# Query and key tiles of the dilated attention: eight pairs by seven block products, six heads' outputs kept in memory outside the core

## The chip, the cores and the metric

The kernel runs on one core of one Trainium2 chip. The core has TensorE (matrix products), VectorE, ScalarE and GpSimd (called POOL in the profile) for elementwise work, and DMA queues, most of them issued from SyncE (SP). The metric is the device time of one execution in microseconds (us); lower is better.

## What is computed

A decoder trunk of two layers on 512 tokens of width 1024 in float32: layer 0 mixes tokens by dilated windowed attention, layer 1 by a state-space scan (Mamba-2), each is followed by a gated feed-forward layer with a short convolution, and all have a normalisation ahead. The change lies in the attention. Cut to that part, the reference is:

```python
qkv = (h @ w_qkv).reshape(bsz, s, N_ATTN_GROUPS, 3, ATTN_HEADS_PER_GROUP, ATTN_HEAD_DIM)
q = apply_partial_rope(qkv[:, :, :, 0], cos, sin)
k = apply_partial_rope(qkv[:, :, :, 1], cos, sin)
v = qkv[:, :, :, 2].astype(jnp.float32)
outs, lses = [], []
for g in range(N_ATTN_GROUPS):
    dil = ATTN_DILATIONS[g]
    o_g, lse_g = dilated_window_attention(q[:, :, g], k[:, :, g], v[:, :, g], dil,
                                          ATTN_WINDOWS[g] // dil)
    outs.append(o_g)
    lses.append(lse_g)
wts = jax.nn.softmax(jnp.stack(lses, axis=2), axis=2)
o = jnp.einsum("bsgh,bsghe->bshe", wts, jnp.stack(outs, axis=2))
return o.reshape(bsz, s, ATTN_OUT_WIDTH).astype(h.dtype) @ w_o
```

There are 3 groups (dilations 1, 4, 16) and 8 heads of 128 channels, so 24 query tiles and 24 key tiles, each 128 channels by 512 tokens, each the product of a 1024 x 128 weight with the normalised input.

## The kernel before, in words

Channels lie on the partitions and tokens along the free axis. A product in float32 is made of three matmuls in the rounded format float32r (`mm3`, lines 136 to 141): weight and input are each split in a high and a low part, and high x high, high x low and low x high are summed in a bank of PSUM. So one projection (`project`, line 147) takes 8 blocks of 128 input channels x 3 = 24 matmuls of 512 columns. The inputs `xh` and `xl` are 8 tiles each of 128 x 512.

`load_unit` brings a weight tile: a DMA from SP into `raw`, a ring of 4 tiles (pool `wr`, line 58), the high part by ScalarE (line 125) and the low part by VectorE (line 126) into `hi` and `lo`, rings of 5 tiles each (pool `wh`, line 59). Transfers and splits thus run some projections ahead of TensorE, as far as the rings are free.

Projections write to three banks of PSUM in turn (`mm_bank`); three more (`aux_bank`) hold transposes and values, and two (`side_bank`) hold scores. `qk_step` (from line 390) takes a query or key tile out of its bank: VectorE multiplies by a table of cosines that also holds the normalisation (line 395), shuffles 32 rows (line 398), and POOL does the sine part (lines 399 and 400).

The order on TensorE is written out by hand in `attend_and_project`: the scores of head h, its value transposes, two projections of head h + 1, the other scores and the join of the softmax pieces over dilations on VectorE (lines 462 to 479), then projections again, with the transposes of the weighted scores (line 488, tile pp, after their scaling on line 485) put behind the second of eight blocks of the sixth projection, and last the values (lines 496 and 501). On the other engines and on SP a planner orders instructions by its own estimate of times. Heads 6 and 7 and the output projection are mixed by the planner on TensorE too.

At the end of a head the output `o` (lines 523 to 525; one buffer) is split in a high and a low tile (lines 526 to 530), which stay until the output projection reads all eight heads. `high_low` (line 81) gives such tiles from two rings of 8.

At the start, `xp` tiles (the input, kept in the ring `v` of 12 tiles with the values) are split into xh and xl, while the first value projections `v_steps` run.

The feed-forward stage already computes its products by seven blocks (`load_sevens`, line 694, and `down_by_sevens`, line 728): two output tiles by two halves of the tokens, with the input blocks paired, are 2 x 2 block products, done with 7 multiplications in place of 8, at the cost of sums of weight blocks, of inputs and of results. Its matmuls have 256 columns.

Of the kernel before, what the change touches and what calls it, by code (L numbers as in the profile page):

```python
# [14 lines left out]
P = 128  # L15
# [16 lines left out]
FF_PARTS = ((0, 8), (8, 8), (16, 6))  # L32

# [18 lines left out]
def trunk(ctx: ExitStack, tc: tile.TileContext, A, out):  # L52
# [244 lines left out]

    vt = {}
# [55 lines left out]
    load2, second = v_steps(2, 0)  # L354
    with tc.manual_schedule(engines={mybir.EngineType.PE}):
        first[3]((0,))
        with tc.manual_schedule(engines={mybir.EngineType.DVE}):
            inv_rms(ssum, D, rcol, soon=True)
            load2(0)
        first[3]((1,))  # L360
        rb = along_free(rcol, "rb")
# [9 lines left out]
    dma(tri, A["tri"])  # L371
    with tc.manual_schedule(engines={mybir.EngineType.PE}):
        for f in second:
            f()
        T.matmul(warm[:, 0:P], ones, ones, start=True, stop=True)
# [26 lines left out]

    def v0_step(h):
        n = f"v0{h}"
        p = project(A["wqk"][h * 7 + 6], n)
        t = t2("t" + n, "vt", 1, s3)
        V.tensor_tensor(in_blocks(t), by_residue(p), by_residue(rbc), op=ALU.mult)
        v0[h] = t
# [9 lines left out]
    def qk_steps(h):  # L418
        steps = [lambda cut=None, g=g, c=c: qk_step(h, g, c, cut) for g in range(NG) for c in range(2)]
        return steps + [lambda: v0_step(h)]  # L420
# [4 lines left out]
    def attend(h):  # L425
# [99 lines left out]
        V.tensor_tensor(natural(o), natural(o), po.rearrange("p (n r l) -> p n r l", n=4, r=DIL), op=ALU.add)  # L525
        o_h, o_l = high_low(f"o{h}")
# [3 lines left out]
        ol.append(o_l)  # L530

# [22 lines left out]
    for f in qk_steps(0):  # L554
        f()
# [17 lines left out]
    for h in range(NH):  # L573
        if h < NH - 2:
            attend_and_project(h)
            if h == 3:
                for f in v_steps(1, 1)[1] + v_steps(2, 1)[1]:
                    f()
# [70 lines left out]
    H0, H1 = slice(0, 256), slice(256, 512)  # L649

# [42 lines left out]

    def load_sevens(src, name):

        def raw(t):
            return wr.tile([P, 1024], F32, tag="raw", name=f"raw{t}_{name}")

        a, b, c = (raw(t) for t in "abc")
        q = t2(f"q_{name}", "a", 13, lp)  # L700
        W0, W1 = slice(0, 512), slice(512, 1024)
        dma(a[:, W0], src[:, 0:512])
        dma(q, src[:, 512:1024])
        dma(b[:, W1], src[:, 1024:1536])
        dma(c[:, W0], src[:, 1536:2048])

        def sums(which=(0, 1)):
            if 0 in which:
                V.tensor_tensor(a[:, W1], q, b[:, W1], op=ALU.add)
                V.tensor_tensor(b[:, W0], a[:, W1], a[:, W0], op=ALU.subtract)  # L710
            if 1 in which:
                V.tensor_tensor(c[:, W1], c[:, W0], b[:, W0], op=ALU.subtract)
                V.tensor_tensor(q, a[:, W0], q, op=ALU.subtract)

        def split_weights(t, between=None):
            r = dict(zip("abcd", (a, b, c, q)))[t]
            hi, lo = (
                wh.tile([P, 1088], F32R, tag=k, name=f"{k}{t}_{name}")[:, 0 : r.shape[-1]] for k in ("hi", "lo")
            )
            SC.copy(hi, r)  # L720
            if between:
                between()
            V.tensor_tensor(lo, r, hi.bitcast(F32), op=ALU.subtract)
            return hi, lo

        return sums, split_weights
# [109 lines left out]
    def ffn(layer, done):  # L836
# [7 lines left out]
        for part, (c0, cn) in enumerate(FF_PARTS):  # L844
# [3 lines left out]
            def load(mp):  # L848
                return load_sevens(A["wds"][(layer * 2 + part) * 4 + mp], f"wd{layer}{part}{mp}")
# [580 lines left out]
def _layout(i):  # L1430
# [9 lines left out]
    w["wqk"] = np.concatenate([qk, v0], 1).reshape(56, P, D)  # L1440
    w["wv"] = (
# [60 lines left out]
```

## Time and profile before

| what | value |
|---|---|
| median of 3 runs | 1611.09 us (1610.67 to 1611.6) |
| the profiled execution | 1610.76 us |
| its span | 1608.8 us |
| TensorE busy | 1601.0 us |
| VectorE busy | 1164.2 us |
| ScalarE busy | 700.7 us |
| POOL busy | 567.9 us |
| granted TensorE clock, mean | 0.999 |
| one head of the attention (134.49 to 180.31 us) | 45.82 us |

In the rows that follow, PE is TensorE's matmuls, PEld its weight loads, DVE VectorE, ACT ScalarE. A row of a group gives line, engine, operation, result and inputs, shapes and count, then the busy time and the mean duration of one in ns, then the idle time of that engine ahead of it. A row of the chain gives start, length and what ran; a row of a stretch gives its bounds, its length and each engine's busy time in it. The profiled execution is 2.0 us longer than its span, which begins with the first and ends with the last instruction that the profile shows.

### The profile page before, as it was taken

What the parts mean: (1) busy time and instruction counts of PE and PEld (TensorE: products, weight loads), DVE (VectorE), ACT (ScalarE), POOL (GpSimd) and SP (SyncE); (2) the same over time, 40 slices, a digit from 0 to 9 for tenths busy, and PEclk for the clock granted to TensorE, in tenths of its full rate; (3) what the DMA queues carried; (4) which work ended last, traced back from release to release, by engine and by line L of the source; (5) the groups of instructions that cost most, each with busy time, mean ns of one, the idle gap of its engine ahead of it and who ended that gap; (6) DMA issues with size and microseconds to landing.
All of it is one profiled execution on the core that took longest, in us unless ns stands there. A gap on an engine that the chain in (4) does not pass through costs nothing.

```text
span 1608.8 us, 22680 instructions
## 1 busy us (share of the span) xinstructions
PE 1601.0 (100%) x8614; PEld 1392.8 (87%) x8614; DVE 1164.2 (72%) x1973; ACT 700.7 (44%) x1077; POOL 567.9 (35%) x432
## 2 busy tenths in 40 slices
PE   9999999999999999999999999999999999999998
PEld 8888888888888889989988888888888888988987
DVE  6366665276646878868758899988898687877864
ACT  5233333333324644443445455544444454444443
POOL 0444453055412653652331222222022285365230
PEclk9999999999999999999999999999999999999999
DMA  7322222222224323423323433233432322342331
GB/s 261 97 76 90 79 79 92 92 92 79 70 88 132 98 64 101 149 61 105 125 92 115 145 114 115 90 114 115 128 128 66 107 84 79 106 129 74 94 129 53
DMA packets 57853, 165.25 MB, mean 103 GB/s; under 512 B 6736, under 2 KB 10192, under 8 KB 57744
## 3 DMA queue, kind: packets, MB, share of 16 engines
q1 hardware_dynamic: 57184, 163.27, 31.5%
q8 instruction: 68, 1.11, 0.3%
q10 hardware_dynamic: 560, 0.53, 0.1%
q14 instruction: 41, 0.34, 0.1%
HBM read 161.62 MB, written 2.16 MB: 102 GB/s over the span
## 4 chain that ended last, share of the span: by engine, by line
PE 98%; DVE 1%; issue 0%; DMA 0%; POOL 0%; ACT 0%; POOLq 0%; DVEq 0%; SPq 0%; ACTq 0%
PE u L134 29%; PE qk L134 16%; PE v L134 8%; PE z L134 5%; PE wso L134 5%; PE xs L134 5%; PE wo L134 3%; PE b L134 3%; PE c L134 3%; PE wd L134 2%; PE wz L134 2%; PE py L1083 1%; PE pg L501 1%; PE pp L488 1%; PE po L496 1%; PE pf L1091 1%
## 5 line engine op out<-in xcount | busy, mean ns | idle before, releaser
L134 PE MATMUL u<-xh,hi_u 128*128 128x512 f32 x704 | 269.4, 383 | 0.0
L134 PE MATMUL u<-xh,lo_u 128*128 128x512 f32 x704 | 269.1, 382 | 0.0
L134 PE MATMUL u<-xl,hi_u 128*128 128x512 f32 x704 | 266.6, 379 | 0.0
L399 POOL TENSOR_TENSOR rotqk<-rotqk,sr 32x512 f32<-32x512 f32 x48 | 92.9, 1936 | 252.6 <-DVE rotqk L398 242.2
L134 PEld LDWEIGHTS u<-xh,lo_u 128*128 128x128 f32 x704 | 131.7, 187 | 24.6
L134 PEld LDWEIGHTS u<-xl,hi_u 128*128 128x128 f32 x704 | 131.7, 187 | 24.0
L126 DVE TENSOR_TENSOR lo_u<-raw_u,hi_u 128x1024 fp32r<-128x1024 f32 x88 | 123.8, 1415 | 37.6 <-ACT hi_u L125 37.6
L134 PEld LDWEIGHTS u<-xh,hi_u 128*128 128x128 f32 x704 | 131.7, 187 | 22.0 <-issue 0.4
L134 PE MATMUL qk<-xh,hi_qk 128*128 128x512 f32 x384 | 148.6, 387 | 0.0
L134 PE MATMUL qk<-xh,lo_qk 128*128 128x512 f32 x384 | 147.1, 383 | 0.0
L134 PE MATMUL qk<-xl,hi_qk 128*128 128x512 f32 x384 | 145.6, 379 | 0.0
L125 ACT CAST hi_u<-raw_u 128x1024 fp32r<-128x1024 f32 x88 | 91.8, 1048 | 106.0 <-PE u L134 65.9
L618 DVE SCALAR_TENSOR_TENSOR au<-u,par,au 128x511 f32<-128x511 f32 (+1 forms) x152 | 113.3, 745 | 20.4 <-ACT au L616 18.0
L643 POOL TENSOR_TENSOR au<-au,au 128x512 f32<-128x512 f32 x43 | 58.1, 1350 | 170.1 <-DVE au L618 156.3
L125 ACT CAST hi_qk<-raw_qk 128x1024 fp32r<-128x1024 f32 x48 | 50.3, 1047 | 130.3 <-PE qk L134 69.3
L1028 POOL TENSOR_TENSOR xdd<-xdt,dec 128x384 f32<-128x384 f32 x16 | 18.0, 1140 | 240.4 <-DVE xdt L1027 240.4
L631 DVE TENSOR_TENSOR u<-u,rbc 128x512 f32<-128x512 f32 x76 | 52.8, 695 | 66.0 <-PE u L134 65.8
L126 DVE TENSOR_TENSOR lo_qk<-raw_qk,hi_qk 128x1024 fp32r<-128x1024 f32 x48 | 62.5, 1302 | 32.0 <-ACT hi_qk L125 32.0
L395 DVE TENSOR_TENSOR qk<-qk,cr 128x512 f32<-128x512 f32 x48 | 33.0, 687 | 72.6 <-PE qk L134 72.4
L134 PEld LDWEIGHTS qk<-xh,lo_qk 128*128 128x128 f32 x384 | 71.8, 187 | 13.3
L134 PEld LDWEIGHTS qk<-xl,hi_qk 128*128 128x128 f32 x384 | 71.9, 187 | 12.8
L134 PEld LDWEIGHTS qk<-xh,hi_qk 128*128 128x128 f32 x384 | 71.9, 187 | 11.2
(2452 smaller groups left out, 4339.3 us busy)
## 6 DMA issues: line engine op xcount, KB each, us to landing
raw_u<-in_wup SPq DMA_DIRECT2D x88, 512.0 KB, 3.4
raw_qk<-in_wqk SPq DMA_DIRECT2D x48, 512.0 KB, 3.3
raw_xs<-in_win SPq DMA_DIRECT2D x16, 512.0 KB, 3.4
raw_z<-in_win SPq DMA_DIRECT2D x16, 512.0 KB, 3.4
lm<-rows SPq DMA_DIRECT2D x32, 256.0 KB, 5.4
raw_wso<-in_wso SPq DMA_DIRECT2D x16, 512.0 KB, 3.3
raw_v<-in_wv SPq DMA_DIRECT2D x12, 512.0 KB, 3.5
raw_wd<-in_wdn SPq DMA_DIRECT2D x16, 384.0 KB, 3.2
```

Source lines behind the costliest of these rows:

```text
L125: SC.copy(hi[:, s], raw[:, s])
L126: low.tensor_tensor(lo[:, s], raw[:, s], hi.bitcast(F32)[:, s], op=ALU.subtract)
L134: T.matmul(in_turns(dst), w, in_turns(x), start=first, stop=last, skip_group_check=skip)
L395: V.tensor_tensor(at(t), of(p), of(cr), op=ALU.mult)
L399: G.tensor_tensor(rot[R, :], rot[R, :], sr[R, :], op=ALU.mult)
L488: T.transpose(pp[:, b * P : (b + 1) * P], pr[:, b * P : (b + 1) * P], ident)
L496: T.matmul(po[:, ii], v0[h][:, b * P : (b + 1) * P], pts[i][:, (b - i + 1) * P : (b - i + 2) * P], start=b == max(i - 1, 0), stop=b == i,)
L501: T.matmul(pg[:, ii], vt[g, half][i][:, es], pts[i][:, (g + 1) * P : (g + 2) * P], start=g == 1, stop=g == 2,)
L618: V.scalar_tensor_tensor(dst[:, j:], src[:, : S - j], col(c_w + taps - 1 - j), dst[:, j:], op0=ALU.mult, op1=ALU.add,)
L631: V.tensor_tensor(dst, p, rbc, op=ALU.mult)
L643: by.tensor_tensor(ab[1], ab[0], ab[1], op=ALU.mult)
L1028: G.tensor_tensor(v4(u[:, 0:384], 3), v4(t[:, 0:384], 3), b3(dec3[:, 0:3, heads[x]], 64), op=ALU.mult)
```

## The change

For eight pairs of a query and a key tile of the same head and group, (0,1), (0,2) and (h,1) for heads 1 to 6, the two projections are replaced by `qk_pair`: seven sets of 4 x 3 matmuls of 256 columns, into quarter results r1 to r4 that use the three projection banks and one bank of the other kind, two of them summed up twice. The weights come as four blocks (a, b, c from the raw ring, q in a tile of another ring), are summed by VectorE (`sums`) and split in four pairs of high and low tiles. The quarters are put together by ScalarE copies and VectorE adds, and `turn` does the cosine and sine part, now from SBUF instead of PSUM.

The combined inputs are made once, at the start, by `combine`, from the xp tiles; their high and low parts fill all 8 tiles of the two rings that held the heads' outputs. The outputs of heads 0 to 5 are therefore written unsplit to memory outside the core (`store`), and after the last pair has been projected, behind head 5, `fetch_heads` reads them back, two to a raw tile, and splits them. The projections of head 0 now have TensorE's order by hand. `load_sevens` is moved up without other change than that its fourth tile is given by the caller; the weights are laid out once more, as `wqs`.

```diff
@@ -30,6 +30,8 @@
+QK_PAIRS = ((0, 1), (0, 2), (1, 1), (2, 1), (3, 1), (4, 1), (5, 1), (6, 1))
+STORED = 6
...
+    def load_sevens(src, name, spare):
+
...
+        a, b, c = (raw(t) for t in "abc")
+        q = spare(f"q_{name}")
+        W0, W1 = slice(0, 512), slice(512, 1024)
+        dma(a[:, W0], src[:, 0:512])
+        dma(q, src[:, 512:1024])
+        dma(b[:, W1], src[:, 1024:1536])
+        dma(c[:, W0], src[:, 1536:2048])
...
+        def sums(which=(0, 1)):
+            if 0 in which:
+                V.tensor_tensor(a[:, W1], q, b[:, W1], op=ALU.add)
+                V.tensor_tensor(b[:, W0], a[:, W1], a[:, W0], op=ALU.subtract)
+            if 1 in which:
+                V.tensor_tensor(c[:, W1], c[:, W0], b[:, W0], op=ALU.subtract)
+                V.tensor_tensor(q, a[:, W0], q, op=ALU.subtract)
+
+        def split_weights(t, between=None):
+            r = dict(zip("abcd", (a, b, c, q)))[t]
+            hi, lo = (
+                wh.tile([P, 1088], F32R, tag=k, name=f"{k}{t}_{name}")[:, 0 : r.shape[-1]] for k in ("hi", "lo")
+            )
+            SC.copy(hi, r)
+            if between:
+                between()
+            V.tensor_tensor(lo, r, hi.bitcast(F32), op=ALU.subtract)
+            return hi, lo
+
+        return sums, split_weights
...
+    minus = sm.tile([P, KD], F32, tag="minus", name="minus", bufs=1)
+    V.tensor_scalar(minus, par[:, C_MIX : C_MIX + KD], -1.0, None, op0=ALU.mult)
+    combined = []
+
+    def combine(j):
+
+        x1, x2 = xps[2 * j], xps[2 * j + 1]
+        w1, w2, m1 = col(C_MIX + 2 * j), col(C_MIX + 2 * j + 1), minus[:, 2 * j : 2 * j + 1]
+        (ah, al), (bh, bl) = high_low(f"ta{j}"), high_low(f"tb{j}")
+        d, t = (t2(f"{n}{j}", "pr", 7, s3) for n in ("d", "t"))
+        e, t4 = d[:, H1], d[:, H0]
+        V.tensor_tensor(d[:, H0], x1[:, H1], x1[:, H0], op=ALU.subtract)
+        SC.activation(e, x2[:, H1], AF.Copy, scale=w2)
+        SC.activation(ah[:, H0], d[:, H0], AF.Copy, scale=w1)
+        V.scalar_tensor_tensor(
+            al[:, H0], d[:, H0], w1, ah[:, H0].bitcast(F32), op0=ALU.mult, op1=ALU.subtract
+        )
+        V.scalar_tensor_tensor(t[:, H0], d[:, H0], m1, e, op0=ALU.mult, op1=ALU.add)
+        V.scalar_tensor_tensor(t[:, H1], x1[:, H1], m1, e, op0=ALU.mult, op1=ALU.add)
+        V.scalar_tensor_tensor(t4, x2[:, H0], w2, t[:, H0], op0=ALU.mult, op1=ALU.subtract)
+        for h, l, at, src in ((ah, al, H1, t[:, H0]), (bh, bl, H0, t[:, H1]), (bh, bl, H1, t4)):
+            SC.copy(h[:, at], src)
+            V.tensor_tensor(l[:, at], src, h[:, at].bitcast(F32), op=ALU.subtract)
+        combined.append(((ah, al), (bh, bl)))
...
+    for j in range(KD // 2):
+        combine(j)
...
+    def turn(t, n):
+
+        rot = t2("rot" + n, "rot", 2, s3)
+        R = slice(0, ROPE)
+        V.stream_shuffle(rot[R, :], t[R, :], SWAP)
+        V.tensor_tensor(t, t, cr, op=ALU.mult)
+        G.tensor_tensor(rot[R, :], rot[R, :], sr[R, :], op=ALU.mult)
+        G.tensor_tensor(t[R, :], t[R, :], rot[R, :], op=ALU.add)
+
+    def qk_pair(h, g):
+
+        n = f"qk{h}{g}"
+        sums, split_weights = load_sevens(
+            A["wqs"][QK_PAIRS.index((h, g))], n, lambda n: t2(n, "sq", 2)
+        )
+        sums()
+        w = {}
+        r1, r3, r2 = (mm_bank(f"{n}r{i}")[:, 0:256] for i in (1, 3, 2))
+        r4 = aux_bank(f"{n}r4")[:, 0:256]
+        kept = t2("kept" + n, "ssum", 2)
+        s1, s5 = kept[:, H0], kept[:, H1]
+        q, k = (t2(f"{n}{c}", "qk", 10, s3) for c in range(2))
+
+        def products(dst, t, at, operand, begin):
+            if t not in w:
+                w[t] = split_weights(t)
+            for j in range(KD // 2):
+                mm3(dst, *w[t], at + j, *operand(j), begin and j == 0, j == KD // 2 - 1, skip=True)
+
+        def plain(b, h):
+            return lambda j: (xh[2 * j + b][:, h], xl[2 * j + b][:, h])
+
+        def other(i, h):
+            return lambda j: [t[:, h] for t in combined[j][i]]
+
+        products(r1, "a", 0, plain(0, H0), True)
+        SC.copy(s1, r1)
+        products(r3, "a", 4, other(0, H0), True)
+        SC.copy(s5, r3)
+        products(r2, "b", 0, other(0, H1), True)
+        V.tensor_tensor(q[:, H1], s1, r2, op=ALU.add)
+        products(r4, "b", 4, other(1, H1), True)
+        products(r1, "c", 0, plain(1, H0), False)
+        SC.copy(q[:, H0], r1)
+        products(r3, "c", 4, plain(1, H1), False)
+        V.tensor_tensor(q[:, H1], q[:, H1], r3, op=ALU.add)
+        turn(q, n + "0")
+        products(r2, "d", 0, other(1, H0), False)
+        V.tensor_tensor(k[:, H0], s1, r2, op=ALU.add)
+        V.tensor_tensor(k[:, H1], k[:, H0], s5, op=ALU.add)
+        V.tensor_tensor(k[:, H0], k[:, H0], r4, op=ALU.add)
+        turn(k, n + "1")
+        qk[h, g, 0], qk[h, g, 1] = q, k
...
     def qk_steps(h):
-        steps = [lambda cut=None, g=g, c=c: qk_step(h, g, c, cut) for g in range(NG) for c in range(2)]
+        steps = []
+        for g in range(NG):
+            if (h, g) in QK_PAIRS:
+                steps += [lambda g=g: qk_pair(h, g), lambda: None]
+            else:
+                steps += [lambda cut=None, g=g, c=c: qk_step(h, g, c, cut) for c in range(2)]
         return steps + [lambda: v0_step(h)]
...
         V.tensor_tensor(natural(o), natural(o), po.rearrange("p (n r l) -> p n r l", n=4, r=DIL), op=ALU.add)
+        if h < STORED:
+            dma(store[h * P : (h + 1) * P, :], o)
+        else:
+            split_head(h, o)
+
+    store = tc.dram_tile([STORED * P, S], F32, name="store")
+
+    def split_head(h, o):
         o_h, o_l = high_low(f"o{h}")
         SC.copy(o_h, o)
         V.tensor_tensor(o_l, o, o_h.bitcast(F32), op=ALU.subtract)
         oh.append(o_h)
         ol.append(o_l)
+
+    def fetch_heads():
+
+        for j in range(STORED // 2):
+            raw = wr.tile([P, 1024], F32, tag="raw", name=f"raw_o{j}")
+            for i in range(2):
+                h = 2 * j + i
+                o = raw[:, i * S : (i + 1) * S]
+                dma(o, store[h * P : (h + 1) * P, :])
+                split_head(h, o)
...
-    for f in qk_steps(0):
-        f()
+    with tc.manual_schedule(engines={mybir.EngineType.PE}):
+        for f in qk_steps(0):
+            f()
...
         if h < NH - 2:
             attend_and_project(h)
+            if h == STORED - 1:
+                fetch_heads()
...
-                return load_sevens(A["wds"][(layer * 2 + part) * 4 + mp], f"wd{layer}{part}{mp}")
+                return load_sevens(
+                    A["wds"][(layer * 2 + part) * 4 + mp], f"wd{layer}{part}{mp}", lambda n: t2(n, "a", 13, lp)
+                )
...
+    blocks = qkv.reshape(4, 2, P, NG, 3, NH, HD)
+    w["wqs"] = np.stack([
+        np.concatenate(
+            [blocks[:, k, :, g, m, h].transpose(1, 0, 2).reshape(P, 512) for m, k in ((0, 0), (1, 0), (1, 1), (0, 1))],
+            axis=1,
+        )
+        for h, g in QK_PAIRS
+    ])
```

More of the change, by code (lines that the diff above doesn't have):

```diff
@@ L295, in down, with raw @@
             finish()
+    H0, H1 = slice(0, 256), slice(256, 512)
+    def load_sevens(src, name, spare):
+        def raw(t):
+            return wr.tile([P, 1024], F32, tag="raw", name=f"raw{t}_{name}")
+        a, b, c = (raw(t) for t in "abc")
[23 more added lines that the diff above has]
+        return sums, split_weights
     vt = {}
@@ L647, in gated @@
         return gate(layer, c, [convolved(layer, i, scaled(layer, i)) for i in (2 * c, 2 * c + 1)])
-    H0, H1 = slice(0, 256), slice(256, 512)
     def split_by(by, high, low, src):
@@ L692, in split_second @@
         return xhl, f, b
[L694 to L726, printed above, removed]
     def down_by_sevens(layer, part, load, sevens, w, finish_pairs, covers, fetch):
```

## The prediction, made before the result was known

> **What bounds the kernel now.** I read the page first, for the shares of the engines and the chain that ended last.
>
> ```profile
> span 1608.8 us, 22680 instructions
> PE 1601.0 (100%) x8614; PEld 1392.8 (87%) x8614; DVE 1164.2 (72%) x1973; ACT 700.7 (44%) x1077; POOL 567.9 (35%) x432
> PE 98%; DVE 1%; issue 0%; DMA 0%; POOL 0%; ACT 0%; POOLq 0%; DVEq 0%; SPq 0%; ACTq 0%
> ```
>
> TensorE is at work for all but 7.8 us of the span and the chain lies on it. So time goes only if TensorE gets less to do, and comes back wherever another engine makes it wait. Next I read the chain in order of time, at one head of the attention (first three rows) and at the feed-forward stage, where this kernel already uses seven block products.
>
> ```profile
> 134.49 10.58 PE qk L134 x48
> ...
> 146.82 17.18 PE qk L134 x78
> ...
> 164.77 4.05 PE qk L134 x18
> 598.36 9.63 PE wd000r L134 x84
> 607.99 10.66 PE u L134 x48
> ...
> 638.93 9.63 PE wd002r L134 x84
> 648.57 9.63 PE wd003r L134 x84
> 658.20 63.46 PE u L134 x288
> ```
>
> Two whole projections are 48 matmuls of 512 columns in 10.58 us, 220 ns from start to start. One set of seven products is 84 matmuls of 256 columns in 9.63 us, 115 ns from start to start. Sets that follow each other (638.93, 648.57, 658.20) leave no gap. A matmul's own duration in the trace is longer, as they overlap, so the sum goes by these pieces of the chain.
>
> Then the busy time of each engine in stretches: the start behind the first projection, one head, in it the stretch from the second scores to the transposes, the feed-forward stretch above, and the start of head 6.
>
> ```profile
> core 0: us, PE busy (x) PEld busy (x) DVE busy (x) ACT busy (x) POOL busy (x), PEclk, DMA share, GB/s
> 28.12:49.72 21.60, 21.60 (x99) 18.21 (x99) 7.60 (x8) 8.47 (x12) 0.00 (x0) 1.00 0.54 183
> 180.31:226.12 45.81, 45.81 (x242) 39.94 (x242) 30.93 (x82) 15.80 (x31) 20.92 (x12) 1.00 0.25 82
> 192.40:209.70 17.30, 17.30 (x82) 14.67 (x81) 15.32 (x52) 5.34 (x12) 6.96 (x4) 1.00 0.20 62
> 598.36:658.20 59.84, 59.84 (x434) 56.48 (x433) 50.48 (x70) 27.17 (x38) 26.08 (x22) 1.00 0.34 106
> ```
>
> A head keeps VectorE at 30.93 of 45.81 us (68%), but at 15.32 of 17.30 (89%) between the second scores and the transposes, where the softmax is joined. The granted clock is 1.00 throughout.
>
> **TensorE's saving.** In each of the eight pairs 48 long matmuls go and 84 short ones come: 10.58 − 9.63 = 0.95 us, and 8 × 0.95 = 7.6 us. The operands differ in place from those of the feed-forward sets (halves of xh and xl, and the combined tiles), not in shape or in the order of weights, so I take the rate from there.
>
> The Trainium skill (TensorE: Matmul & The Clock Gate, "Wait — 56ns, not 53.3ns?") gives a warm matmul its columns over 2.4 GHz and a fixed 2.5 ns or so. By it 48 × 215.8 ns stand against 84 × 109.2 ns, 10.36 against 9.17 us, and the eight pairs would save 9.5 us. The rows show 220 and 115 ns, about 7 and 8 ns over 512 and 256 columns at that clock: the fixed part is larger here and the short matmuls pay it more often, so the rows decide.
>
> **VectorE's and ScalarE's new work, per pair.** These groups hold the prices:
>
> ```profile
> L126 DVE TENSOR_TENSOR lo_qk<-raw_qk,hi_qk 128x1024 fp32r<-128x1024 f32 x48 | 62.5, 1302 | 32.0 <-ACT hi_qk L125 32.0
> L723 DVE TENSOR_TENSOR loc_wd<-rawc_wd,hic_wd 128x1024 fp32r<-128x1024 f32 x16 | 28.1, 1758 | 0.0
> L723 DVE TENSOR_TENSOR loa_wd<-rawa_wd,hia_wd 128x1024 fp32r<-128x1024 f32 x16 | 23.6, 1478 | 0.0
> L723 DVE TENSOR_TENSOR lob_wd<-rawb_wd,hib_wd 128x1024 fp32r<-128x1024 f32 x16 | 19.4, 1215 | 0.0
> L723 DVE TENSOR_TENSOR lod_wd<-q_wd,hid_wd 128x512 fp32r<-128x512 f32 x16 | 14.0, 873 | 0.0
> L712 DVE TENSOR_TENSOR rawc_wd<-rawc_wd,rawb_wd 128x512 f32<-128x512 f32 x16 | 13.1, 821 | 0.3
> L709 DVE TENSOR_TENSOR rawa_wd<-q_wd,rawb_wd 128x512 f32<-128x512 f32 x16 | 11.2, 697 | 0.0
> L398 DVE STREAM_SHUFFLE rotqk<-qk 32x512 f32<-32x512 f32 x48 | 35.2, 733 | 0.0
> L395 DVE TENSOR_TENSOR qk<-qk,cr 128x512 f32<-128x512 f32 x48 | 33.0, 687 | 72.6 <-PE qk L134 72.4
> ```
>
> Out go two low parts, 2 × 1.30 = 2.60. In come four low parts (1.76 + 1.48 + 1.22 + 0.87 = 5.33), four sums of weight blocks (0.82 + 3 × 0.70 = 2.92) and five adds of 256 columns. The multiplication by the cosines and the shuffle stay, one of each for a projection (0.69 and 0.73). An add of 256 columns costs 0.41:
>
> ```profile
> 610.27 1.22 DVE L723 TENSOR_TENSOR loa_wd<-rawa_wd,hia_wd 128x1024 fp32r<-128x1024 f32 x1
> 611.40 0.41 DVE L822 TENSOR_TENSOR xr<-xr,wd000r 128x256 f32<-128x256 f32 x1
> ```
>
> So VectorE gets 5.33 − 2.60 + 2.92 + 5 × 0.41 = 7.7 us more in a pair. A head's split of its output, about 0.7 at L395's rate, moves away, so a head comes to 30.93 + 7.0 = 37.9 of 45.81 − 0.95 = 44.86 us, 84%. That is the load at which the feed-forward stretch ran without a gap (50.48 of 59.84, 84%). ScalarE, at 15.80, has room for three half-width copies and wider high parts, and POOL's two instructions per projection stay.
>
> The tight place is the stretch of 17.30 us, now 0.95 shorter, 16.35. What must be done there before the transposes is what is there now, 15.32 (one turn of a projection among it, which can wait), and the two adds that free the banks of the next products (2 × 0.41): 16.14, just in time. Put ahead as well, the other three adds (1.23) and a second turn (1.42) make 18.79 and a wait of 2.4. So each of heads 0 to 5 may lose 0 to 2.4 us; I take 0.2, near the lower end, as the turns and k's adds are wanted only by the next head. Six heads: 1.2.
>
> **Weights.** The raw ring of four gives three to a pair and the ring of five high and low tiles gives four, in two kinds each. Tile d of a pair needs the slot of the projection two before it, c the one before that; each is free one projection of 5.3 us before the pair begins, and d is first wanted 8.3 us into it. The four loads carry the bytes of two. I take nothing; if that cover went, a pair would wait for a sum, a high and a low part, 0.7 + 1.05 + 1.3 = 3.1 us (the high part's row stands below).
>
> **The start.** `combine` adds 4 × 8 VectorE operations of half width, 32 × 0.41 = 13.1 us, and 20 on ScalarE. The second set of value projections can leave its banks at 49.72 only when two of the four are done (the x tiles share its ring): 7.60 + 6.6 = 14.2 of 21.60 us. The others are due with the first pair, two projections (10.6 us) later. Bounds 0 to 2 us, the latter if they push aside the low parts; I take 0.4, by the idle time of that row.
>
> **Outputs by way of memory.** A store waits in SP's queue for o; behind it are weight loads, which have several tiles of 5.3 us each in hand. The tile o is wanted again a head later. Heads 0 to 4 have landed long before they are fetched. Head 5's has a short path:
>
> ```profile
> 405.46 1.15 DVE L525 TENSOR_TENSOR o<-o,po 128x512 f32<-128x512 f32 x1 [0.51 <-ACT o L524]
> ```
>
> ```profile
> 413.34 14.08 PE qk L134 x64
> ```
>
> ```profile
> L125 ACT CAST hi_qk<-raw_qk 128x1024 fp32r<-128x1024 f32 x48 | 50.3, 1047 | 130.3 <-PE qk L134 69.3
> ```
>
> ```profile
> out<-ot SPq DMA_DIRECT2D x3, 256.0 KB, 2.5
> xr<-in_xt SPq DMA_DIRECT2D x8, 256.0 KB, 4.0
> raw_qk<-in_wqk SPq DMA_DIRECT2D x48, 512.0 KB, 3.3
> ```
>
> The sum ends at 406.6; store 2.5, fetch up to 4.0, two splits 2 to 4 (VectorE joins at that time), then the freed raw tile takes the fourth projection's weights, 3.3, and their split, 1.05 and 1.30: 417 to 423 with 0 to 2 us of queueing, so up to 425. The fourth projection begins 48 matmuls after 413.34, at 423.9. Bounds 0 to 1.1 us, and nothing can be gained here; I take 0.4, between the ends. The moved splits, six times, fall into heads 6 and 7.
>
> **The sum.** 7.6 − 1.2 − 0.4 − 0.4 = 5.6 us. The profiled execution took 1610.76 (span 1608.8 and 2.0 around it), so 1605.2 on its scale; the median of the runs lies 0.3 above it: 1605.5.
>
> **Rival one, slower: VectorE becomes the bound of the attention.** Place: between the second scores and the transposes of each of six heads. If all of the pair's later work goes ahead of the join, the wait is 2.4 us a head, 14.4 in all: from the median of before, 1611.1 − 7.6 + 14.4 + 0.8 = 1619. POOL can make it worse; the same low part, alone and beside POOL:
>
> ```profile
> 192.84 1.86 DVE L126 TENSOR_TENSOR lo_v<-raw_v,hi_v 128x1024 fp32r<-128x1024 f32 x1
> ```
>
> ```profile
> 193.69 2.14 POOL L400 TENSOR_TENSOR qk<-qk,rotqk 32x512 f32<-32x512 f32 x1
> ```
>
> Alone it took 1.22 (row at 610.27). The turn now multiplies from SBUF instead of PSUM, and with the sums there are some eight more operations exposed to this; four of them in the stretch at 0.65 each add 2.6 a head, 15.6 in all: 1634. It decides from a wait of 7.6 / 6 = 1.3 us a head. For it speaks the 89% of that stretch; against it that most of the added work need not be there.
>
> The Trainium skill (SBUF — State Buffer, "Who interferes with whom") says that a VectorE instruction with two SBUF inputs contends with a GpSimd one that reads SBUF, and the later one waits. The two rows above agree with it; it makes this rival dearer but does not place the work.
>
> **Rival two, no change: the outputs come back in one piece.** If no row of the store can be read before head 5's is in, the first three raw tiles are all held past 409.1. The second projection of head 6, at 413.34, then waits for fetch (3 to 4), split (2), load (3.3) and split (2.35), until about 420: 6.8 us. Total 1611.1 − 7.6 + 1.6 + 6.8 = 1611.9. For it: all six share one tensor in memory. Against it: the rows are disjoint, and halves of one raw tile are already written and read apart.
>
> **Rival three, faster still:** the skill's rate without any wait, 1611.1 − 9.5 = 1601.6; the rows at 115 ns speak against it.
>
> **Chances.** About 0.2% (3.2 us) is what a measurement of this kernel can tell from no change, so faster is under 1607.9 and slower above 1614.3. Forecast with its smaller waits 0.70 (1603.5 with no wait to 1607.8), rival three 0.02, rival two and partial losses like it 0.17, rival one 0.11. Faster 0.72, same 0.17, slower 0.11. The range runs from 1603.0 (no wait, and half a microsecond for a changed order elsewhere) to 1610.5: it leaves out rivals one and three and the upper part of two, about 0.2.
>
> **What would show it.** Pieces of the chain: 84 matmuls in about 9.6 us at each pair, heads 0 to 5 about 44.9 to 45.1 us long. VectorE near 38 us a head. A pp row behind an idle TensorE waiting for L485 would show rival one; a gap before head 6's second projection rival two, before its fourth my fetch term; one at 50 to 62 us the start. The forecast is wrong if a set takes over 10.2 us, or if heads come out longer than 45.8.

## The result, and the profile after

The changed kernel takes 1698.46 us (median of 4 runs, 1697.02 to 1700.38) against 1610.99 us (4 runs, 1610.67 to 1611.6): 87 us more, a ratio of 1.0543 with a 95% interval of 1.0525 to 1.0561. The forecast was 1605.5. First the page of the kernel after, the span, the engines and the chain:

```profile
span 1697.4 us, 23559 instructions
...
PE 1625.3 (96%) x8902; PEld 1416.5 (83%) x8902; DVE 1235.5 (73%) x2094; ACT 727.5 (43%) x1137; POOL 578.7 (34%) x432
...
PE 87%; DVE 9%; issue 2%; DMA 1%; ACT 1%; POOL 0%; SPq 0%; DVEq 0%; POOLq 0%; ACTq 0%
```

The chain, 98% on TensorE before, now has 9% on VectorE. TensorE's busy time has grown by 24 us although it has less to do, which points to a lower clock. The two largest of TensorE's waits, after (total, times, longest):

```profile
PE pp L612 <- DVE pr L609: 50.3, 18, 7.8
PE sc L571 <- POOL qk L475: 7.2, 1, 7.2
```

The kernel before had no such row for pp: TensorE's longest wait there was 1.1 us, at the start. It is the row that the prediction had named as the sign of its first rival: the transposes wait for the scaling of the scores. The chain through one head of the kernel after, and the stretches around the stop:

```profile
166.90 10.66 PE qk L136 x48
...
179.31 3.85 PE qk21r L136 x34
...
202.43 3.51 DVE pr L609 x3
205.99 1.12 PE pp L612 x4
207.10 6.10 PE qk L136 x18
...
224.78 1.38 PE qk L136 x6
```

```profile
core 0: us, PE busy (x) PEld busy (x) DVE busy (x) ACT busy (x) POOL busy (x), PEclk, DMA share, GB/s
3.70:32.00 28.30, 22.81 (x92) 17.88 (x90) 27.43 (x60) 22.93 (x44) 0.00 (x0) 0.91 0.69 242
166.90:224.78 57.88, 48.73 (x278) 42.80 (x278) 37.13 (x92) 17.67 (x35) 22.28 (x12) 0.88 0.20 69
179.31:207.10 27.79, 18.64 (x122) 16.62 (x122) 25.82 (x64) 8.62 (x18) 14.39 (x7) 0.83 0.26 86
```

A head takes 57.88 us instead of 45.82. VectorE's 37.13 us in it are what had been forecast (37.9), but 25.82 of them lie in the 27.79 us between the second scores and the first transposes, and there TensorE stands for 27.79 − 18.64 = 9.15 us (7.65 in one piece from 195.67 to 203.32, then 0.86 and 0.64). Behind that stop TensorE has work without a break, and is slow: the 18 matmuls at 207.10 take 6.10 us, where the kernel before needed 4.05 (the row at 164.77 in the prediction). Why the scaling L609 comes so late is seen in VectorE's own queue, in order of time:

```profile
188.56 0.16 DVE L594 TENSOR_TENSOR join<-own,oth 128x8 f32<-128x8 f32 x1
188.64 1.22 DVE L128 TENSOR_TENSOR lo_v<-raw_v,hi_v 128x1024 fp32r<-128x1024 f32 x1
189.77 0.16 DVE L595 TENSOR_TENSOR join<-own,join 128x8 f32<-128x8 f32 x1
...
191.16 1.20 DVE L128 TENSOR_TENSOR lo_qk<-raw_qk,hi_qk 128x1024 fp32r<-128x1024 f32 x1
192.28 1.23 DVE L598 TENSOR_TENSOR join<-own,join 128x8 f32<-128x8 f32 x1
...
195.05 1.21 DVE L128 TENSOR_TENSOR lo_qk<-raw_qk,hi_qk 128x1024 fp32r<-128x1024 f32 x1
196.19 0.15 DVE L600 TENSOR_TENSOR join<-join 128x8 f32<-128x8 f32 x1
...
196.60 0.67 DVE L318 TENSOR_TENSOR rawb_qk<-rawa_qk 128x512 f32<-128x512 f32 x1
197.20 0.67 DVE L321 TENSOR_TENSOR q_qk<-rawa_qk,q_qk 128x512 f32<-128x512 f32 x1
197.80 0.18 DVE L601 RECIPROCAL join<-join 128x8 f32<-128x8 f32 x1
...
199.40 0.62 DVE L602 TENSOR_TENSOR join<-join 128x8 f32<-128x8 f32 x1
199.95 1.21 DVE L331 TENSOR_TENSOR loa_qk<-rawa_qk,hia_qk 128x1024 fp32r<-128x1024 f32 x1
...
202.34 4.90 DVE L609 TENSOR_SCALAR pr<-pr,join 128x128 f32<-128x128 f32 x8
```

The join is a chain of eight small operations, L594 to L602, most of which need the one before. Between most of them stands something long that was ready: low parts of weights, sums of weight blocks (L317 to L321), the pair's adds. The chain takes 188.56 to 200.02, 11.5 us, and the scaling begins 2.3 us after it, behind a low part and two shuffles. VectorE doesn't idle, it does other work first, the pair's and the next head's.

The kernel before had the same pattern in small (a turn's shuffle and a low part stood between the steps), with room for it:

```profile
201.17 0.16 DVE L470 TENSOR_TENSOR join<-own,oth 128x8 f32<-128x8 f32 x1
...
206.04 0.17 DVE L478 TENSOR_TENSOR join<-join 128x8 f32<-128x8 f32 x1
206.25 2.13 DVE L485 TENSOR_SCALAR pr<-pr,join 128x128 f32<-128x128 f32 x8
```

Its chain took 5.0 us, and the scaling was done at 208.38, 1.3 us before TensorE began the transposes (209.66).

By place, from the starts of the heads in the two traces, the 88.6 us that the span grew are 20.4 ahead of the first one (109.06 against 88.67), 65.1 in six heads (some 12 in five of them, 6 in the fourth) and 3.1 in the rest.

### The profile page after: what moved, and what is told of

It is laid out like the page before. It is cut to its first block, busy times and chain, and to the rows that moved or that the text cites. A ratio compares the mean times of both kernels' runs of the same rounds, so it can differ in the third digit from the quotient of the medians.

```text
span 1697.4 us, 23559 instructions
## 1 busy us (share of the span) xinstructions
PE 1625.3 (96%) x8902; PEld 1416.5 (83%) x8902; DVE 1235.5 (73%) x2094; ACT 727.5 (43%) x1137; POOL 578.7 (34%) x432
## 4 chain that ended last, share of the span: by engine, by line
PE 87%; DVE 9%; issue 2%; DMA 1%; ACT 1%; POOL 0%; SPq 0%; DVEq 0%; POOLq 0%; ACTq 0%
PE u L136 28%; PE qk L136 8%; PE v L136 6%; PE xs L136 5%; PE wso L136 5%; PE z L136 5%; PE b L136 3%; PE c L136 3%; PE wo L136 3%; PE wd L136 2%; PE wz L136 2%; DVE pr L609 1%; PE pp L612 1%; PE py L1195 1%; DVE oth L591 1%
## 5 line engine op out<-in xcount | busy, mean ns | idle before, releaser
L128 DVE TENSOR_TENSOR lo_u<-raw_u,hi_u 128x1024 fp32r<-128x1024 f32 x88 | 124.3, 1422 | 38.6 <-ACT hi_u L127 38.5
L464 POOL TENSOR_TENSOR rotqk<-rotqk,sr 32x512 f32<-32x512 f32 x32 | 54.2, 1694 | 224.5 <-DVE rotqk L463 214.1
L764 DVE SCALAR_TENSOR_TENSOR au<-u,par,au 128x511 f32<-128x511 f32 (+1 forms) x152 | 113.4, 746 | 20.4 <-ACT au L762 18.0
L136 PE MATMUL qk<-xh,hi_qk 128*128 128x512 f32 x256 | 105.0, 410 | 0.1
L136 PE MATMUL qk<-xh,lo_qk 128*128 128x512 f32 x256 | 102.0, 398 | 0.0
L136 PE MATMUL qk<-xl,hi_qk 128*128 128x512 f32 x256 | 101.8, 398 | 0.0
L460 DVE TENSOR_TENSOR qk<-qk,cr 128x512 f32<-128x512 f32 x32 | 22.0, 687 | 83.3 <-PE qk L136 83.2
L612 PE MATMUL pp<-ident,pr 128*128 128x128 f32 x120 | 24.0, 334 | 50.3 <-DVE pr L609 50.3
L762 ACT ACTIVATE au<-u,par 128x512 f32<-128x512 f32 x76 | 59.1, 778 | 23.0 <-DVE u L777 21.4
L612 PEld LDWEIGHTS pp<-ident,pr 128*128 128x128 f32 x120 | 16.0, 165 | 57.5 <-DVE pr L609 55.8
L239 POOL TENSOR_TENSOR ssum<-ssum,sq 128x512 f32<-128x512 f32 x21 | 32.5, 1549 | 84.4 <-ACT sq L238 84.0
L940 POOL TENSOR_TENSOR xr<-xr,sums 128x512 f32<-128x512 f32 x16 | 33.1, 2068 | 82.1 <-DVE sums L938 82.1
```

What stands on the lines that cost most here:

```text
L128: low.tensor_tensor(lo[:, s], raw[:, s], hi.bitcast(F32)[:, s], op=ALU.subtract)
L136: T.matmul(in_turns(dst), w, in_turns(x), start=first, stop=last, skip_group_check=skip)
L239: add.tensor_tensor(ssum, ssum, sq, op=ALU.add)
L460: V.tensor_tensor(at(t), of(p), of(cr), op=ALU.mult)
L464: G.tensor_tensor(rot[R, :], rot[R, :], sr[R, :], op=ALU.mult)
L612: T.transpose(pp[:, b * P : (b + 1) * P], pr[:, b * P : (b + 1) * P], ident)
```

## The experiments

My theory was that VectorE's order costs the time, at the start and in each head, not the amount of its work. The main rival was that 37 us a head, beside POOL, are too many for any order. A kernel keeps every operation of the change where nothing else is said. Other places in VectorE's queue come from a block (`issue_after`) that puts the VectorE instructions traced in it behind a given one. "Head" is from one piece of two projections to the next, the second such span of each kernel (before: 45.82).

**Storing alone, and combine alone.** `e_store` projects every tile by itself again and leaves combine out; `e_comb` puts combine back, and nothing reads what it makes.

```diff
-QK_PAIRS = ((0, 1), (0, 2), (1, 1), (2, 1), (3, 1), (4, 1), (5, 1), (6, 1))
+QK_PAIRS = ()
...
```

and in `e_store` alone:

```diff
-    for j in range(KD // 2):
-        combine(j)
```

> The changed kernel without any pair and without combine: only the outputs of heads 0 to 5 go by way of memory, and head 0's projections have TensorE's order by hand. Theory (the loss is VectorE's order, at two places): this part is near free, 1609 to 1614 us. Rival (the outputs come back too late for head 6): a gap of several us at the start of head 6, 1616 us or more.

> The same with combine at the start, whose results nobody reads. Theory: the planner puts combine's 32 VectorE operations between the first splits and the sum of squares, so the second set of value projections begins 8 to 11 us later (38 instead of 28 us): 1619 to 1624 us, and nothing else moves. Rival (combine fits into VectorE's idle time, as the prediction had it): 1610 to 1613 us, and the start's loss belongs to the pairs.

Measured: 1615.78 and 1625.92 us, one run each, beside 1611.31. Heads are 46.07 and 46.08, so neither stops them; combine costs 10.1 us, as its theory had it, all of it at the start (the whole lies above the theory's band, as `e_store` does above its own). Storing came out between theory and rival: a head has no stop, but two projections took 10.66 us where they had taken 10.58 (below, under addresses).

**combine later.** In the kernel after, VectorE was busy for 27.43 of the 28.30 us from 3.70 on (the row above), with combine's operations between those that the sum of squares needs. `e_late` is the changed kernel with combine queued behind the first operation after that sum.

```diff
-            inv_rms(ssum, D, rcol, soon=True)
+            mean = inv_rms(ssum, D, rcol, soon=True)
...
-    for j in range(KD // 2):
-        combine(j)
+    with tc.issue_after(mean.ins):
+        for j in range(KD // 2):
+            combine(j)
```

> The changed kernel with combine's VectorE operations queued behind the operation that follows the sum of squares. Theory: the first 8 to 11 us of the loss go, 1687 to 1691 us; the heads stay at 57 to 58 us. Rival (combine's amount costs wherever it stands): the delay shows up between 28 and 62 us instead, 1696 us or more.

Measured: 1689.94 us (one run), 8.5 less, as expected; the head stays at 57.95. So some 8.5 of combine's 10.1 us are its place in the queue.

**The join ahead of the next head's work.** `e_order` is the changed kernel, with what is traced between the first scores of a head and its transposes queued behind the scaling of the head before, and what is traced behind the transposes behind this head's own.

```diff
-                V.tensor_scalar(pr[:, cs], pr[:, cs], share[:, w, i : i + 1], None, op0=ALU.mult)
+                scaled[:] = [V.tensor_scalar(pr[:, cs], pr[:, cs], share[:, w, i : i + 1], None, op0=ALU.mult)]
...
+            with behind():      # tc.issue_after(scaled[0].ins)
                 next(core)
                 v0_turn(h)
...
                 fill[5](cut=(2, lambda: next(core)))
+            with behind():
                 next(core)
                 fill[6]()
                 next(core, None)
```

> The changed kernel with one change of order: what VectorE does for weights and projections traced behind the scaling of the first two score tiles is queued behind that scaling. The same instructions run, none is left out. Theory (order): the stop of 11 us ahead of the transposes goes, a head takes 45 to 47 us instead of 57.9, total 1632 to 1645 us (the start still loses 20). Rival (amount: VectorE or its contention with POOL is the bound of a head): heads stay above 52 us, total above 1665 us.

Measured: 1664.46 us (one run), 34 less, the head 53.60: neither band, with the head in the rival's. VectorE's queue at the same place in a head:

```profile
183.85 0.16 DVE L594 TENSOR_TENSOR join<-own,oth 128x8 f32<-128x8 f32 x1
...
186.13 0.14 DVE L602 TENSOR_TENSOR join<-join 128x8 f32<-128x8 f32 x1
...
187.20 3.84 DVE L609 TENSOR_SCALAR pr<-pr,join 128x128 f32<-128x128 f32 x8
```

The same chain takes 2.4 us now instead of 11.5, and the scaling ends when TensorE comes to the transposes. But the low parts that had been in its way now stood ahead of the turns of the pair's key and the last key, these came late to POOL, and the wait was at the next scores (the single wait of 8.7 us is another one, ahead of head 0's first scores):

```profile
PE sc L571 <- POOL qk L465: 12.8, 4, 3.2
PE sc L571 <- POOL qk L475: 8.7, 1, 8.7
PE sc L570 <- POOL qk L475: 6.5, 4, 1.7
```

**The turns ahead too.** `e_order2` has combine as in `e_late`, the next head's low parts and pair behind the shuffle of this head's last turn, and the value's low part behind the pair's last cosine product. `e_order2_head0` gives head 0 four projections again.

```diff
+            with behind(last):       # shuffle of this head's last turn
                 next(core)
                 v0_turn(h)
                 fill[0]()
                 fill[1]()
+            with behind(last):
                 next(core)
                 next(core)
                 fill[2]()
...
+            with behind(paired):     # cosine product of the pair's key
                 fill[6]()
```

> The changed kernel, every operation of it kept, with VectorE's queue set by hand in three places: combine stands behind the operation after the sum of squares (as in e_late); of each head, the next head's first two low parts and the next pair's sums and low parts stand behind the shuffle of this head's last turn; and the value's low part stands behind the multiplication of the pair's key. Theory (the amount of VectorE's work fits, its order does not): both stops of a head go, that ahead of the transposes and that ahead of the next scores, and a head takes 45 to 47.5 us instead of 57.9; the whole 1615 to 1632 us. Rival (37 us of VectorE work a head, with POOL beside it, leaves no order in which every wait is met): a stop of over 3 us remains or appears elsewhere in each head, heads at 50 us or more, the whole 1645 or more.

> As e_order2, and the two pairs of head 0 go back to four projections; six pairs are left. Theory (two pairs one behind the other leave POOL's turn of the second one late, and the first scores wait for it): the wait ahead of the first scores falls from about 10 us to under 2, TensorE has 2 us more to do, and the whole is 6 to 10 us under e_order2, 1607 to 1624 us. Rival (the wait of the start belongs to combine alone, and is paid already by queueing it later): within 2 us of e_order2 or above it.

Measured: 1640.49 us (4 runs, 1639.83 to 1645.16; the trace is of the longest), and 1636.83 without head 0's pairs. The whole and the head (49.91) both lie between theory and rival. Both stops are gone; a third one is there, and the wait of head 0, which its second pair brings, stays:

```profile
PE pv L535 <- DVE tv L528: 12.4, 4, 3.2
PE sc L573 <- POOL qk L477: 8.7, 1, 8.7
```

tv is the value of the head. In the second head the last matmul of its product began at 189.91, and VectorE came to tv at 196.06: it stood behind four sums and two low parts. Without head 0's pairs its wait falls from 8.7 to 0.8 us, as the theory had it, but the whole by 3.7 only by the medians, under the 6 to 10 expected (by the two profiled executions 8.3), and it stayed above the band of 1607 to 1624.

**The value ahead too.** `e_order3` queues the next pair's sums and low parts behind tv. `e_order3_gap` also puts combine's 8 negated weights into a tile of 8 that the kernel allocates and doesn't use, so nothing behind them moves. `e_order3_gap_h0` is this without head 0's pairs.

```diff
-            with behind(last):
+            with behind(list(weighed)):   # weighting of this head's value, tv
                 next(core)
                 next(core)
                 fill[2]()
...
-    cp.tile([P, 8], F32, tag="gap", name="gap")
+    minus = cp.tile([P, 8], F32, tag="gap", name="minus")
...
-    minus = sm.tile([P, KD], F32, tag="minus", name="minus", bufs=1)
```

> As e_order2, with one thing more: the sums and low parts of the next head's pair stand behind the weighting of this head's value (tv), which in e_order2 stood behind them and held the turn of the value by 3.2 us a head. Theory (order): no stop of over 1 us is left in a head but head 0's wait of 8.7 us for its second pair; a head goes from 50.2 us to 45 to 46.5 us, the whole from 1640.5 to 1609 to 1620 us. Rival (VectorE and POOL side by side are too slow for any order; the low parts moved now delay the next scores or the pair itself): a stop of 2 us or more remains in each head, heads at 48 us or more, the whole 1627 or more.

> As e_order3, and the 8 negated weights lie in a tile of 8 that the kernel allocates and doesn't use, so that the tiles behind lie where they lay before the change. Theory (addresses set the 222 ns against 220 ns of a long matmul, as e_store_tile showed with 3.7 us): 3 to 4.5 us under e_order3. Rival (the gain of e_store_tile belongs to something else that the tile's operation did): within 1 us of e_order3.

> As e_order3_gap, with the two pairs of head 0 back at four projections, six pairs left. Theory: 8 us of wait at the first scores go, 2 us of TensorE work and about 2 to 3 us of other waits come, as between e_order2 and its like, so 3 to 4.5 us under e_order3_gap: 1601 to 1612 us, which is under the kernel before (1611.1) if the heads are at 45.5 or less. Rival (a head with a pair can't come under one without, since what VectorE has to do more takes the TensorE time back): 1613 us or more.

Measured: 1617.70 (1615.65 to 1618.19), 1612.37 (1610.87 to 1614.56) and 1612.03 us (1611.13 to 1613.43), against 1611.52. `e_order3` is in its theory's band, and the order alone has brought back 1698.46 − 1617.70 = 81 of the 87 us. The chain of `e_order3_gap` through its first head, and its second head as a stretch:

```profile
91.62 10.59 PE qk L136 x48
...
103.97 9.71 PE qk11r L136 x84
113.68 6.74 PE qk L136 x30
120.42 0.77 PE pp L613 x7
121.18 4.01 PE qk L136 x18
...
136.68 3.32 PE qk L136 x15
```

```profile
136.68:181.78 45.10, 45.10 (x279) 40.68 (x278) 38.94 (x92) 17.27 (x36) 21.31 (x12) 1.00 0.28 88
```

This row settles the rival: VectorE does 38.94 us in a head of 45.10, more than in the kernel after, and TensorE is at work all the time at a granted clock of 1.00. What is left of the saving is 45.82 − 45.10 = 0.72 us a head. The gap tile gave 5.3 us (3 to 4.5 expected). That head 0's pairs cost 3 to 4.5 us is not shown: the medians differ by 0.3, within their ranges, and 1612.03 lies between theory and rival. The wait that the expectation wanted to save, 8.7 us in `e_order2`, was down to 2.3 us in `e_order3_gap`.

**Addresses.** `e_store_tile` is `e_store` without the tile of negated weights and the operation that fills it; all that is allocated later lies 32 bytes lower. `e_gap` is the changed kernel with that tile in the unused one, and its order as it was.

> The kernel e_store (no pairs, no combine; outputs of six heads by way of memory) without the tile of 8 negated weights and its one operation, so that all tiles allocated after it lie 32 bytes lower in each partition. Theory (the 222 ns a matmul of e_store's projections, against 220 in the kernel before, come from where the operands lie): projections back at 10.58 us a pair, heads at 45.8, the whole 1611 to 1613.5 us. Rival (they come from the traffic of stored outputs, or from the order of head 0): unchanged within 1 us of e_store's 1615.8.

> The changed kernel as it is, with only the 8 negated weights moved into the unused tile of 8, so that what lies behind keeps its addresses; VectorE's order is left as the change has it. Theory (two causes that add: addresses 3 to 5 us over the whole kernel, order the rest): 1692 to 1696 us. Rival (the rate of matmuls sets nothing while VectorE's order stops TensorE anyway): within 1.5 us of 1698.5.

Measured: 1612.03 us (10 runs) against 1615.78, and 1695.98 (1695.2 to 1697.86) against 1698.46. The same piece in `e_store` and in `e_store_tile`:

```profile
135.18 10.66 PE qk L136 x48
```

```profile
134.76 10.58 PE qk L136 x48
```

222.1 and 220.4 ns a matmul. The tile's place sets it (in `e_order3_gap` the operation is still there), and storing itself costs nothing that can be measured (ratio of `e_store_tile` to before 1.0007, interval 0.9997 to 1.0017). In the changed kernel it is worth 2.5 us: the whole is inside the band, the gain under the 3 to 5 us expected.

**Bringing the outputs back.** With the heads at 45.1, head 5 still took 49.4 us in `e_order3_gap` and 47.7 in `e_order3_gap_h0`: low parts of the fetched outputs stood between the steps of its join. `e_fetch8` and `e_fetch6` queue them behind head 6's tv (eight and six pairs); `e_back6` traces the fetching a head later and queues it behind head 6's scaling.

```diff
             if h == STORED - 1:
-                fetch_heads()
+                with behind(list(weighed)):    # e_fetch8, e_fetch6
+                    fetch_heads()
...
+        if h == NH - 2:                        # e_back6, instead
+            with behind(scaled):
+                fetch_heads()
```

> As e_order3_gap (all eight pairs), and what brings the outputs of heads 0 to 5 back is queued on VectorE behind the weighting of head 6's value; in e_order3_gap the low parts of these outputs stood between the steps of the joining of head 5, which took 49.4 us where the others took 45.1. Theory (order again, at this place too): head 5 at 45.1 to 46 us, and the whole 3 to 4 us under e_order3_gap's 1612.4: 1607 to 1610 us. Rival (the low parts are in the way wherever they stand, in head 6's joining now): within 1 us of e_order3_gap.

> As e_order3_gap_h0 (six pairs), with the same placing of what brings the outputs back. Theory: head 5 falls from 47.7 to 45.1 to 45.5 us, the whole from 1612.0 to 1608.5 to 1610.5 us, under the kernel before (1611.5) by about what a measurement can tell; six pairs at 0.7 us each, 4.3 us, less about 2 us that combine, the storing and head 6 cost. Rival: within 1 us of 1612.

> As e_order3_gap_h0 (six pairs), but the outputs of heads 0 to 5 are brought back one head later: their fetches, high parts and low parts are traced behind the joining of head 6, and the low parts are queued on VectorE behind head 6's scaling. Theory (in e_fetch6 head 5 gained 2.2 us and head 6 lost more, since o5's low part and late low parts pushed the joining of head 6 beside POOL's turns; where there is a free stretch behind the scaling, both are met): head 5 at 45.1 to 45.7 us, from head 6's start to the output projection 67 to 69 us, the whole 1607 to 1610.5 us, under the kernel before. Rival (the bringing back costs 2 to 5 us wherever it lies): 1612 us or more.

Measured: 1618.55, 1616.92 and 1611.72 us, the last against 1611.68, ratio 1.0000 with an interval of 0.9991 to 1.0009. The first two are misses on both sides. Head 5 did come down (head 6 starts 2.2 us earlier in `e_fetch6` than in `e_order3_gap_h0`), but its waits and VectorE's queue in head 6 show a new stop there:

```profile
PE pp L613 <- DVE pr L610: 4.6, 3, 3.2
```

```profile
421.13 4.79 DVE L592 COPY oth<-own 32x4 f32<-32x4 f32 x16
...
429.84 4.18 DVE L610 TENSOR_SCALAR pr<-pr,join 128x128 f32<-128x128 f32 x8
```

The 16 copies take 4.79 us where they took 2.81 in `e_order3_gap_h0`, the scaling 4.18 where it took 2.13: both fell beside POOL's turns. In `e_back6` the longest such wait is 1.1 us, and the chain runs through the storing and fetching instead:

```profile
404.82 1.18 DVE o L650
...
406.02 3.21 DMA store<-o
...
409.24 2.53 DMA raw_o<-store
...
412.32 1.05 ACT hi_qk L127
...
413.40 1.76 DVE lo_qk L128
```

Head 5's output goes out and back in 6 us, ScalarE's queue waits for it, and weights that head 6 needs stand behind it. Against the kernel before, head 5 starts 2.9 us earlier (357.55 against 360.46) and the output projection only 0.7 (472.83 against 473.53); the rest, 0.9 us longer, was not followed up. At 1611.72, `e_back6` lies between its theory's 1610.5 and its rival's 1612, nearer the rival: no version beat the kernel before by what can be measured. Whether still another place would was not tried.

## Why the prediction was wrong

**TensorE's saving held, a little smaller.** A set took 9.71 us, not 9.63, and a head came to 0.72 us less instead of 0.95, where nothing made it wait.

**VectorE's amount held.** 37.13 us a head against 37.9. That such a load can run without a gap was right too, as the head with 38.94 of 45.10 us (86%) shows.

**The step that failed is the one on the tight stretch**: "What must be done there before the transposes is what is there now, 15.32 ... and the two adds ...: 16.14, just in time", and 0.2 us a head taken for it. It counted what has to be done there and took for granted that this is what will be done there. VectorE works its queue in the order that the planner wrote, and the planner filled most gaps of the join's chain with long work. The stretch it was read from already held that pattern: the 15.32 us had two low parts among them, 3.07 us that the transposes didn't need. A head lost 57.88 − 45.10 = 12.8 us: 9.15 of standing, and the rest, some 3.6, in matmuls at a lower clock behind the stop, which no term of the sum had. The bound of 2.4 us was a bound on the pair's own work; the next head's low parts and sums were not in it.

**"Weights. I take nothing"** was right on the question it asked, whether loads and slots come in time, and missed what the slots do. A pair uses four high and low slots in 9.7 us, so several come free in one pair, where in the kernel before one came free each 5.3 us. The low parts and sums of the next projections (L128 at 188.64, 191.16 and 195.05, L317 to L321, L331 at 199.95) ran just while the join did. That the slots brought them there is read from the code and these rows; no run varied the rings.

**combine** was placed in the idle time of 28.12 to 49.72 by the reader, not by the planner, which began it at 3.7 us, ahead of the sum of squares: 10.1 us instead of 0.4, of which later queueing returns 8.5. That the two pairs of head 0 come one behind the other, and the first scores wait up to 8.7 us for the second one's turn, was not in the sum at all.

**Outputs.** 0.4 us was taken; the storing as such costs nothing measurable. With the heads right, the time from the start of head 5 to the output projection, where the outputs come back, was 2.2 (`e_back6`) to 8.4 us (`e_fetch8`) longer than before.

**Rival one had the place, and the sign to look for, and too small a price**: 2.4 to 5.0 us a head by amounts, against 12.8. What had been held against it, that most of the added work need not be there, is true and didn't help. Rivals two and three were not what happened.

The row at 1.00 of the feed-forward stretch, with VectorE at 84%, gave a false comfort: there, as its code has it, no chain of small operations that TensorE waits for runs through the queue. The load of an engine says how much fits, and nothing about what stands first.

## What to carry to other kernels

Where one engine's queue holds both a chain of small dependent steps that another engine waits for and long work that is ready early, price the order and not the sum: count each step as itself plus the longest ready operation that can stand ahead of it (the chain took 11.5 us here, 5.0 in the kernel before and 2.4 in `e_order`). Before adding work to such an engine, look which buffers come free together, since that is when it can become ready, and pin the chain by hand; each stop that goes (transposes, next scores, value, bringing back) may show the next. Then set what remains of the saving, here 0.7 us a head, against the costs of making room for it.

## What the runs showed of the hardware

**The clock behind a stop.** In the kernel after, around the end of the stop of 7.65 us:

```profile
202.43:207.10 4.67, 2.28 (x8) 1.59 (x9) 4.67 (x9) 0.48 (x1) 3.27 (x3) 0.50 0.26 98
207.10:213.20 6.10, 6.10 (x21) 4.88 (x20) 0.74 (x2) 0.72 (x2) 1.26 (x1) 0.65 0.00 0
```

The granted clock is 0.50 and then 0.65, and the chain's 18 matmuls from 207.10 on took 6.10 instead of 4.05 us (the row counts three more that reach into its stretch). A stop of 3.2 us (7.45 − 4.27, in the first of these stretches of `e_order2`) lowers the clock too:

```profile
190.00:197.45 7.45, 4.27 (x35) 4.00 (x34) 7.42 (x8) 4.12 (x4) 2.03 (x2) 1.00 0.41 130
197.45:211.45 14.00, 14.00 (x63) 11.76 (x62) 6.51 (x22) 4.23 (x11) 3.20 (x3) 0.88 0.39 118
```

The next stretch has a granted clock of 0.88, so the stop cost about 14.00 × 0.12 = 1.7 us more. The Trainium skill (TensorE: Matmul & The Clock Gate, "What's actually happening") has the array fall to half its clock after an idle window of about 3.4 us. The 0.50 of the first row agrees; the stop in `e_order2` was a little shorter than that window.

**32 bytes of address.** A tile of 32 bytes a partition, allocated ahead of others, made long matmuls 222.1 ns instead of 220.4, 2.5 to 5.3 us in all. Which operand's place it is was not tested.

**VectorE beside POOL.** The same eight scalings took 2.13, 3.84 and 4.90 us in different places. The Trainium skill (SBUF — State Buffer, "Who interferes with whom") has copies and products with a scalar among the operations that can contend, under conditions on their operands, for the ports that VectorE shares with GpSimd. The rows agree: the longer times, also those of the 16 copies of 32 x 4 (4.79 us against 2.81), fall beside POOL's turns, and the 2.13 beside none; no run here took POOL's work away to show it.
